# A decoder layer in split fp32: the pool of small tiles is opened last, and three other pools start 8,896 bytes lower

## The chip, the cores and the metric

The kernel runs on one core of a Trainium2 chip. The metric is device time in microseconds (us), from the launch to the end of the program; lower is better. Engine names in the rows: PE is the matmul stream of TensorE, PEld its stream of weight loads, DVE is VectorE, ACT is ScalarE, POOL is GpSimd, SP is SyncE, which issues most DMAs.

## What is computed

One layer of a decoder in float32 for 512 tokens of width 2048. The parts that matter here are the matrix products; every one of them has both operands in on-chip memory (SBUF):

```python
q_a, k_a, v_a, q_b, k_b, v_b = jnp.split(h @ w_in[l], splits, axis=-1)
o_a = swa_sink_attention(q_a, k_a, v_a, sinks[l])       # 16 heads, window 128
o_b = stick_breaking_attention(q_b, k_b, v_b)           # 16 heads, causal
mix = jnp.concatenate([rms(o_a), rms(o_b)], axis=-1) @ w_o[l]
h = layer_norm(ALPHA * h + mix, ln1_g[l], ln1_b[l])
c = memory_cross_attention(h, mem, w_q_mem[l], w_kv_mem[l], w_o_mem[l])
h = layer_norm(ALPHA * h + c, ln2_g[l], ln2_b[l])
gate, up = jnp.split(h @ w_gate_up[l], 2, axis=-1)
f = (jax.nn.silu(gate) * up) @ w_down[l]
h = layer_norm(ALPHA * h + f, ln3_g[l], ln3_b[l])
```

## The kernel before, in words

**Split products.** Each float32 operand is split into a high and a low part of type fp32r (`split`, line 121: ScalarE casts the high part, VectorE subtracts it). A product is then three matmuls, high by high, high by low and low by high (`mm3`, line 143; `product`, line 1032). In each matmul one operand is stationary (128 columns, brought in by a weight load on PEld) and the other one moves through the array (512 or 256 columns). In the rows the moving operand stands first and the stationary one second: `zz<-dn_0h,s2l` is a moving weight tile and a stationary block of activations.

**Stages, in program order.** Values of both attention groups (0 to 120 us; weights move, the input is stationary); attention, with the projections of queries and keys run between its pieces (120 to 530; the input moves, weights are stationary); memory values and keys (530 to 735; 256 columns, weights stationary); the output projection and the values through `w_o_mem` (735 to 1010; weights move); cross-attention (1010 to 1192: `keys` makes a key tile `kq` with `kth` or `ktl` moving and a weight stationary, and `scores` has `kq` move over the stationary hidden state `h1`); its output and the first gate and up blocks (1192 to 1360; weights move); gate and up with seven block products in place of eight (1360 to 2256; weights move); down (2256 to 2686; weights move); and the last layer norm.

**Weight units.** A unit is 128 rows of 4,096 bytes: SP fetches it into a tile `ws`, and `split` makes `wh` and `wl` of it, three buffers of each (pool `pw`). From 735 us on nearly every unit feeds 12 matmuls of 512 columns. Counted from the loops, 7,464 matmuls of 512 columns have a weight tile moving (384 for the values, 768 for `w_o`, 384 through `w_o_mem`, 384 for the output of cross-attention, 5,544 on line 1039), 1,248 have the input moving over a stationary weight tile, and 384 are scores of cross-attention. Of 256 columns there are 2,904: 1,536 for memory, 768 in `keys`, 192 values, 408 in attention.

**What sets the order.** PE and SP run in the order of the program; the order on the other engines comes from the recording layer and its priorities. All waits are on semaphores.

**Where tiles lie.** Pools take their addresses in the order in which they are opened, each after the one before; within a pool each tag has its buffers one after another. The addresses below are bytes within a partition, read from the built programs; the last columns are the first address's remainder on division by 256. Every tile of `px`, `pm`, `pt`, `pg` and `pw` is a multiple of 2,048 bytes long, so all buffers of a pool have the remainder of its first.

| pool (tiles) | first address before | after | remainder before | after |
|---|---|---|---|---|
| `px` (input, `h1`, memory, blocks `a11`, `s2`, ...) | 19744 | 19744 | 32 | 32 |
| `pm` (`kq`, `kth`, values, blocks `a22`, `s1`, ...) | 85280 | 85280 | 32 | 32 |
| `sm` (small tiles and four of 2,048 bytes) | 142624 | 220448 | 32 | 32 |
| `pt` (transposed scores, running sums) | 151520 | 142624 | 224 | 32 |
| `pg` (queries and keys, `ktl`, weight sums) | 176096 | 167200 | 224 | 32 |
| `pw` (`ws`, `wh`, `wl`) | 192480 | 183584 | 224 | 32 |

Of the kernel before, what the change touches and what calls it, by code (L numbers as in the profile page):

```python
# [62 lines left out]
def layer(ctx, tc, io, out):  # L63
# [4 lines left out]
    const = ctx.enter_context(tc.tile_pool(name="const", bufs=1))  # L68
    px = ctx.enter_context(tc.tile_pool(name="px", bufs=4))
    pm = ctx.enter_context(tc.tile_pool(name="pm", bufs=14))  # L70
    sm = ctx.enter_context(tc.tile_pool(name="sm", bufs=2))
    pt = ctx.enter_context(tc.tile_pool(name="pt", bufs=2))
    pg = ctx.enter_context(tc.tile_pool(name="pg", bufs=4))
    pw = ctx.enter_context(tc.tile_pool(name="pw", bufs=3))
    banks = ctx.enter_context(ExitStack())

    def open_banks(k):
# [1343 lines left out]
```

## Time and profile before

| | us |
|---|---|
| median of three runs (2705.70 to 2710.08) | 2708.28 |
| the profiled execution, its own time | 2712.35 |
| the profiled execution, span from first to last instruction | 2710.6 |
| PE busy | 2614.7 |
| DVE busy | 1921.9 |
| ACT busy | 1204.2 |
| mean granted TensorE clock | 0.984 |

The median is 4.07 us below the profiled execution. A row of the timeline gives the start of an instruction (us from the span's start), its length, its engine, line, operation and operands. Matmuls overlap in the pipeline, so the pace of PE is the distance between starts, not the length of one.

### The profile page before, as it was taken

How to read it: one execution, taken by the hardware profiler on the slowest of the kernel's cores; microseconds unless marked ns; L12 is line 12 of the kernel's file. 1: busy time of each engine (PE TensorE's matmuls, PEld its weight loads, DVE VectorE, ACT ScalarE, POOL GpSimd, SP SyncE). 2: the span in 40 equal slices, each digit the busy share in tenths (PEclk: the TensorE clock that was granted, in tenths of full speed). 3: DMA queues.
4: the chain of work that ended last, by engine and by line, in shares of the span. 5: the costliest groups of instructions: out<-in, count | busy, mean ns of one | idle time of the engine just before them, and what ended most of it. 6: DMA issues, size and time to landing. Idle time of an engine off the chain costs nothing.

```text
span 2710.6 us, 33637 instructions
## 1 busy us (share of the span) xinstructions
PE 2614.7 (96%) x13024; PEld 2158.8 (80%) x13024; DVE 1921.9 (71%) x2223; ACT 1204.2 (44%) x1608; POOL 212.3 (8%) x324
## 2 busy tenths in 40 slices
PE   9999999999999999999998989999999998999995
PEld 7877777799988889988777767777778877888884
DVE  4258888896523564457887878778787767777788
ACT  3246666664411353334544444444455443333332
POOL 0001110110000000000101101011111011000001
PEclk9999999999999999999999989999999999999998
DMA  5322222355742573236745546554554568787662
GB/s 180 102 83 70 75 74 71 101 161 190 241 141 96 197 268 107 92 134 210 229 159 212 206 172 214 189 179 152 189 195 168 182 228 312 265 318 261 254 253 102
DMA packets 131264, 476.58 MB, mean 176 GB/s; under 512 B 16160, under 2 KB 16416, under 8 KB 128672
## 3 DMA queue, kind: packets, MB, share of 16 engines
q1 hardware_dynamic: 107568, 391.58, 42.1%
q0 software_dynamic: 23536, 82.85, 8.3%
q8 instruction: 102, 1.67, 0.2%
q14 instruction: 58, 0.48, 0.1%
HBM read 401.49 MB, written 72.88 MB: 175 GB/s over the span
## 4 chain that ended last, share of the span: by engine, by line
PE 70%; issue 14%; DVE 8%; ACT 3%; DMA 2%; POOL 2%; SPq 0%; POOLq 0%; DVEq 0%; ACTq 0%
PE zz L1039 30%; PE ge L1039 2%; POOL f_d L1151 1%; PE kq L147 1%; PE mvp L146 1%; DVE a L351 1%; PE mvp L148 1%; PE vo L148 1%; PE mvp L147 1%; PE kq L148 1%; PE vo L146 1%; PE vo L147 1%; PE kq L146 1%; PE pjqa L146 1%; PE pjqa L148 1%
## 5 line engine op out<-in xcount | busy, mean ns | idle before, releaser
L122 ACT CAST dn_1h<-dn_1a 128x1024 fp32r<-128x1024 f32 x44 | 46.3, 1052 | 76.9 <-PE zz L1039 75.2
L122 ACT CAST dn_0h<-dn_0a 128x1024 fp32r<-128x1024 f32 x44 | 46.3, 1052 | 73.1 <-PE zz L1039 69.1
L123 DVE TENSOR_TENSOR dn_1l<-dn_1a,dn_1h 128x1024 fp32r<-128x1024 f32 x44 | 53.7, 1221 | 23.2 <-ACT dn_1h L122 23.2
L123 DVE TENSOR_TENSOR dn_0l<-dn_0a,dn_0h 128x1024 fp32r<-128x1024 f32 x44 | 53.3, 1221 | 20.0 <-ACT dn_0h L122 20.0
L1161 POOL DMA_DIRECT2D f_d<-fa x22 | 15.8, 716 | 590.6 <-DVE fa L123 590.6
L1151 POOL DMA_DIRECT2D f_d<-fl x66 | 47.1, 714 | 143.4 <-DVE fl L123 140.8
L351 DVE TENSOR_TENSOR_SCAN a<-ones,nl 128x128 f32<-128x128 f32 (+3 forms) x64 | 49.8, 812 | 10.0 <-POOL nl L348 9.9
L122 ACT CAST fh<-fs 128x512 fp32r<-128x512 f32 x44 | 27.2, 619 | 58.3 <-DVE fl L123 42.5
L1151 POOL DMA_DIRECT2D f_d<-fh x66 | 47.2, 715 | 23.7 <-ACT fh L122 20.7
L348 POOL TENSOR_SCALAR_AFFINE_SELECT nl<-nl 128x256 f32<-128x256 f32 x32 | 19.8, 619 | 346.5 <-DVE nl L347 346.5
L1139 PE MATMUL ftr<-ident,f 128*128 128x128 f32 x176 | 26.3, 288 | 16.8 <-DVE fl L123 16.8
L354 ACT ACTIVATE a<-a 128x256 f32<-128x256 f32 (+3 forms) x32 | 23.7, 739 | 39.9 <-DVE a L353 39.9
L123 DVE TENSOR_TENSOR fl<-fs,fh 128x512 fp32r<-128x512 f32 x44 | 30.3, 688 | 14.6 <-DMA f_d<-fl 10.0
L122 ACT CAST dn_1h<-dn_1b 128x1024 fp32r<-128x1024 f32 x22 | 23.2, 1053 | 38.5 <-PE zz L1039 36.7
L1139 PEld LDWEIGHTS ftr<-ident,f 128*128 128x128 f32 x176 | 22.1, 149 | 21.8 <-issue 18.9
L123 DVE TENSOR_TENSOR wmk_0l<-wmk_0s,wmk_0h 128x1024 fp32r<-128x1024 f32 x16 | 19.6, 1226 | 27.6 <-ACT wmk_0h L122 27.5
L122 ACT CAST dn_0h<-dn_0b 128x1024 fp32r<-128x1024 f32 x22 | 23.2, 1053 | 33.4 <-PE zz L1039 29.8
L146 PE MATMUL mkp<-mh,wmk_0h 128*128 128x256 f32 x128 | 36.4, 284 | 1.3 <-DVE ktl L123 1.3
L420 ACT ACTIVATE sa<-sa,nm 128x256 f32<-128x256 f32 x64 | 32.0, 501 | 12.3 <-DVE nm L418 12.2
L146 PE MATMUL mvp<-mh,wmv_1h 128*128 128x256 f32 x128 | 36.7, 287 | 0.0
L146 PE MATMUL mvp<-mh,wmv_0h 128*128 128x256 f32 x128 | 36.4, 285 | 0.0
L824 POOL DMA_DIRECT2D vo_d<-vos x16 | 8.5, 533 | 350.6 <-ACT n1mv L741 277.1
(2465 smaller groups left out, 9743.7 us busy)
## 6 DMA issues: line engine op xcount, KB each, us to landing
f_d<-fh POOLq DMA_DIRECT2D x66, 256.0 KB, 2.8
f_d<-fl POOLq DMA_DIRECT2D x66, 256.0 KB, 2.8
dn_0s<-in_w_dn SPq DMA_DIRECT2D x33, 512.0 KB, 6.9
dn_1s<-in_w_dn SPq DMA_DIRECT2D x33, 512.0 KB, 5.1
wmv_0s<-in_w_mv SPq DMA_DIRECT2D x16, 512.0 KB, 3.5
wmv_1s<-in_w_mv SPq DMA_DIRECT2D x16, 512.0 KB, 3.3
wmk_0s<-in_w_mk SPq DMA_DIRECT2D x16, 512.0 KB, 3.4
wmk_1s<-in_w_mk SPq DMA_DIRECT2D x16, 512.0 KB, 4.2
```

Source lines behind the costliest of these rows:

```text
L122: nc.scalar.copy(hi, src)
L123: return nc.vector.tensor_tensor(lo, src, f32(hi), op=ALU.subtract)
L146: nc.tensor.matmul(acc, lh, rh, start=first, stop=False)
L147: nc.tensor.matmul(acc, lh, rl, start=False, stop=False)
L148: nc.tensor.matmul(acc, ll, rh, start=False, stop=last)
L348: nc.gpsimd.affine_select(out=nlt[:, :, dg], in_=nlt[:, :, dg], compare_op=ALU.is_gt, fill=0.0, base=0, channel_multiplier=1, pattern=[[0, ...
L351: nc.vector.tensor_tensor_scan(a[:, h, :nk][:, ::-1], ones.to_broadcast([P, nk]), nlt[:, h, :nk][:, ::-1], 0.0, op0=ALU.mult, op1=ALU.add)
L354: nc.scalar.activation(a[:, :, :nk], a[:, :, :nk], AF.Exp)
L420: nc.scalar.activation(s4[:, i], s4[:, i], AF.Exp, bias=nm[:, i:i + 1], accum_out=rs[:, i:i + 1])
L1039: nc.tensor.matmul(acc[:, t], l[:, cs(t, P)], r, start=first and c == 0 and i == 0, stop=last and c == 1 and i == 2, skip_group_check=True)
L1139: nc.tensor.transpose(bank[k][:, cs(t, P)], self.f[:, t, o:o + P], ident)
L1151: nc.gpsimd.dma_start(f_d[chunk, b:b + 2, k].rearrange("b p n -> p b n")[:, :, cs(slot, 256)], f32(pieces(v)))
```

## The change

The line that opens the pool `sm` is moved behind the three pools `pt`, `pg` and `pw`. `sm` is 8,896 bytes long (four tiles of 2,048, and small ones), so these three start 8,896 bytes lower, and `sm` starts 77,824 bytes higher.

```diff
     const = ctx.enter_context(tc.tile_pool(name="const", bufs=1))
     px = ctx.enter_context(tc.tile_pool(name="px", bufs=4))
     pm = ctx.enter_context(tc.tile_pool(name="pm", bufs=14))
-    sm = ctx.enter_context(tc.tile_pool(name="sm", bufs=2))
     pt = ctx.enter_context(tc.tile_pool(name="pt", bufs=2))
     pg = ctx.enter_context(tc.tile_pool(name="pg", bufs=4))
     pw = ctx.enter_context(tc.tile_pool(name="pw", bufs=3))
+    sm = ctx.enter_context(tc.tile_pool(name="sm", bufs=2))
     banks = ctx.enter_context(ExitStack())
```

No instruction is added, taken away or moved: on each of the five engines the two built programs have the same instructions in the same order with the same waits on the same semaphores and values, buffer for buffer. The addresses in the table above are all that differs.

## Rows read from the trace of the kernel before

**Rows 1.** The page's part 1: busy time and share of each engine.

```profile
span 2710.6 us, 33637 instructions
PE 2614.7 (96%) x13024; PEld 2158.8 (80%) x13024; DVE 1921.9 (71%) x2223; ACT 1204.2 (44%) x1608; POOL 212.3 (8%) x324
```

**Rows 2.** Stretches of the span: busy time of each engine, granted clock, DMA.

```profile
core 0: us, PE busy (x) PEld busy (x) DVE busy (x) ACT busy (x) POOL busy (x), PEclk, DMA share, GB/s
0.00:530.00 530.00, 514.91 (x2736) 417.03 (x2737) 372.43 (x540) 274.65 (x496) 39.20 (x73) 0.99 0.28 92
530.00:1010.00 480.00, 478.25 (x2915) 421.24 (x2914) 277.67 (x352) 202.11 (x271) 18.21 (x27) 1.00 0.56 184
1010.00:1192.00 182.00, 182.00 (x1190) 166.69 (x1189) 74.78 (x99) 63.22 (x101) 0.53 (x1) 1.00 0.34 111
1192.00:1360.00 168.00, 165.22 (x747) 132.64 (x746) 134.02 (x180) 86.28 (x118) 11.23 (x18) 1.00 0.64 212
1360.00:2256.00 896.00, 853.18 (x3653) 682.95 (x3654) 703.96 (x710) 414.06 (x458) 106.90 (x153) 0.97 0.54 192
2256.00:2686.00 430.00, 421.10 (x1792) 338.27 (x1790) 340.14 (x315) 159.30 (x158) 26.12 (x45) 0.99 0.69 253
```

**Rows 3.** Timeline of PE where scores end and their use begins.

```profile
1184.69 0.39 PE L146 MATMUL s1a<-kq_6h,h1h 128*128 128x512 f32 x1
...
1192.62 0.39 PE L148 MATMUL s1b<-kq_7h,h1l 128*128 128x512 f32 x1
1192.85 0.39 PE L146 MATMUL pvo_0a<-wvo_0h,pmh 128*128 128x512 f32 x1
...
1195.65 0.39 PE L146 MATMUL pvo_0b<-wvo_0h,pmh 128*128 128x512 f32 x1
```

**Rows 4.** Timeline of PE in the down stage.

```profile
2400.16 0.40 PE L1039 MATMUL zz<-dn_1l,a22h 128*128 128x512 f32 x1
...
2404.82 0.40 PE L1039 MATMUL zz<-dn_1h,a22h 128*128 128x512 f32 x1
```

**Rows 5.** Timeline of PE in the first key projection.

```profile
124.88 0.40 PE L148 MATMUL pjkb<-xh,wkb_0l 128*128 128x512 f32 x1
...
127.92 0.40 PE L146 MATMUL pjkb<-xh,wkb_1h 128*128 128x512 f32 x1
```

**Rows 6.** Timeline of PE at two places of the memory stage, 256 columns.

```profile
599.65 0.28 PE L146 MATMUL mvp<-mh,wmv_0h 128*128 128x256 f32 x1
...
601.35 0.28 PE L146 MATMUL mvp<-mh,wmv_0h 128*128 128x256 f32 x1
...
649.99 0.28 PE L148 MATMUL mkp<-mh,wmk_0l 128*128 128x256 f32 x1
...
651.99 0.28 PE L147 MATMUL mkp<-ml,wmk_0h 128*128 128x256 f32 x1
```

**Rows 7.** Timeline of PE in a `keys` block, 256 columns.

```profile
1107.95 0.29 PE L147 MATMUL kq<-ktl,wmq_1h 128*128 128x256 f32 x1
1108.08 0.28 PE L148 MATMUL kq<-kth,wmq_1l 128*128 128x256 f32 x1
...
1110.33 0.28 PE L146 MATMUL kq<-kth,wmq_1h 128*128 128x256 f32 x1
```

**Rows 8.** Groups of splits on ACT and DVE: count, busy us, mean ns, idle before.

```profile
L122 ACT CAST fh<-fs 128x512 fp32r<-128x512 f32 x44 | 27.2, 619 | 58.3 <-DVE fl L123 42.5 <-DMA f_d<-fh 15.8
L122 ACT CAST xh<-x4s 128x512 fp32r<-128x512 f32 x2 | 1.1, 618 | 0.6 <-DMA x4s<-in_xT 0.6
L123 DVE TENSOR_TENSOR dn_1l<-dn_1a,dn_1h 128x1024 fp32r<-128x1024 f32 x44 | 53.7, 1221 | 23.2 <-ACT dn_1h L122 23.2
L123 DVE TENSOR_TENSOR a22l<-hr,a22h 128x1024 fp32r<-128x1024 f32 x2 | 2.4, 1220 | 0.0
```

**Rows 9.** Waits of PE: total us, times, longest; first and last of 21.

```profile
PE ftr L1139 <- DVE fl L123: 16.8, 8, 3.8
...
PE ge L1039 <- DVE wge_1l L123: 0.2, 1, 0.2
```

## The prediction, made before the changed kernel ran

> **What bounds the kernel now.** I read the busy shares first: PE is busy for 2614.7 of 2710.6 us, the next engine, DVE, for 71% [rows 1]. By stretches PE fills each stage, and its clock is granted in full nearly everywhere [rows 2]. The waits of PE, 21 groups, come to 67.2 us in all [rows 9]. So the time is the number of matmuls times the distance between their starts, plus some 67 us of waits and the last layer norm. The instruction streams are the same in both kernels, so nothing can change but how long an access takes at another address. I therefore went to the timeline of PE and measured the distance between starts where no wait intervenes, in pairs of places that differ in where the operands lie.
>
> What a reader should see there: the distance is not one number. In the scores of cross-attention 35 matmuls of 512 columns take from 1184.69 to 1192.62, 7.93 us, or 226.6 ns each; the very next ones, of the same shape and with no wait between, take 12 steps from 1192.85 to 1195.65, 2.80 us, or 233.3 ns each [rows 3]. In the down stage 20 steps take 4.66 us, 233.0 ns [rows 4]. The clock is not the difference: both were granted full clock, that is 2.4 GHz [rows 2, 3], where 6.67 ns are 16 cycles. Nor is traffic: the cross-attention stretch has a DMA share of 0.34, and the down stretch, no slower than the quiet place at 1192.85, has 0.69 [rows 2]. What does differ is the place of the operands. In the scores both `kq` (pool `pm`) and `h1` (pool `px`) begin at remainder 32 of 256 bytes. In the two slower places the moving weight tile is in `pw`, at remainder 224, and the stationary one at 32. With the roles turned round, input moving at 32 over a weight tile at 224, 13 steps take 3.04 us, 233.8 ns [rows 5]. For 256 columns there are two levels with the same operands' remainders (32 moving, 224 stationary): 15 steps in 1.70 us, 113.3 ns, and 17 in 2.00 us, 117.6 ns [rows 6]; the level changes where other pieces have come between.
>
> **The change part by part.** After it `pw`, `pg` and `pt` begin at remainder 32 like `px` and `pm`, so every matmul with a weight tile has both operands at 32, as the scores have now. The multiples of 128 columns at which the stationary slices begin occur in the scores in the same way.
>
> (a) 7,464 matmuls of 512 columns with weights moving. The granted clock of 0.97 and 0.99 in the last two stretches [rows 2] stands for some 2 x (27 + 4) = 62 us at half clock, 1.2 GHz, room for 130 matmuls or so of 427 ns (512 columns, worked out); these I leave out, and call the rest 7,300. Bounds: 0, if remainders do not matter, and 7,300 x 6.67 ns = 48.7 us of gain, if they run at the pace of the scores; the other side is under the rivals. The nearest row is that of the scores, which have after the change's remainders already [rows 3]. I take 48.7.
>
> (b) 1,248 matmuls of 512 columns with the input moving over weights. At the slow pace of rows 5 they could gain 1,248 x 7 = 8.7 us; between the pieces of attention the same operands reach both levels, as for 256 columns in [rows 6]. I take half, 4.3 us, with ends 0 and 8.7.
>
> (c) 2,904 matmuls of 256 columns. They gain at most 117.6 - 113.3 = 4.3 ns each, 12.5 us [rows 6]. The bound on the other side is in `keys`: there a moving `ktl` at 224, with the next weight load also at 224, takes 130 ns by the two starts, against a mean of 119 over 20 steps [rows 7]; at that price all 2,904 would lose some 12 x 2,904 = 35 us. Remainders both at 32 are those of the scores, not of this row, so I take a gain of 5 us.
>
> (d) The other engines. A split of 512 elements takes ACT 619 ns with all tiles at 32 (`fh`) and 618 with the source at 224 (`xh`); one of 1,024 takes DVE 1221 ns with all at 224 (`dn_1l`) and 1220 with all at 32 (`a22l`) [rows 8]. So the moved tiles cost DVE and ACT nothing, and `sm`, whose remainder stays, nothing either. DMAs into `pw` move the same 4,096 bytes per row, and are ahead of their use; I put them at 0, and what they could cost is in (e).
>
> (e) What is late next. A faster PE meets the waits earlier. In gate and up DVE is busy for 704 of 896 us, 79% [rows 2], and the largest waits of PE are for it [rows 9]. Of the 34 to 35 us that (a) gives in those stages and in down (5,256 matmuls x 6.67 ns) I let a seventh go back into waits: a loss of 5 us, with ends 0 and all 35.
>
> Sum against the profiled execution's own time: 2712.35 - 48.7 - 4.3 - 5 + 5 = 2659.4; the median of the runs lies 4.07 lower than that execution, so **2655 us**, 2.0% faster.
>
> A rule speaks against the whole of (a). The Trainium skill, page "SBUF — State Buffer", section "Specifications (TRN2)", gives the memory 16-byte lines and prices only the crossing to a new line; 32, 224 and 8,896 are multiples of 16, so by it every tile begins at a line's start before and after, and the sum would be zero: 2708 us. The trace does not agree with it as the only rule, since it has 226.6 and 233.3 ns for operands that all begin at a multiple of 16 [rows 3].
>
> **The rivals.** *No change, 2708 us.* The two levels may follow not the remainder but the region: everything in `pw` lies above 192,000 bytes before and above 183,000 after, and the scores are the only long products without an operand in the upper pools. Each slow place fits that as well as it fits the remainder, and no row tells them apart. Against it: the fast level does occur with a weight tile in the upper region, in the first pair of [rows 6], and scores run at one pace whichever buffers of `px` and `pm` they use. Time 2700 to 2712. By the page's rule above this would be the result; the row that contradicts that rule does not exclude the region.
>
> *The gain is swallowed where other engines set the pace, 2684 us.* If gate, up and down are held by DVE and DMA, only the 7,464 - 5,256 = 2,208 other matmuls of (a) gain, 14.7 us, with (b) 4.3 and (c) 5: 24 us in all. For: 79% of DVE and a DMA share of 0.69 [rows 2]. Against: PE is busy for 95% and 98% of those stretches, so it is not being held.
>
> *Slower, 2767 us.* Equal remainders collide: with both streams of PE at the same offset the weight load meets the moving reads, as the pair at 224 in `keys` shows with some 10 to 12 ns more than its neighbours [rows 7], in about half of its cases there. At 10.4 ns in half of all, (7,300 + 1,248 + 2,904) / 2 x 10.4 ns = 59.6 us of loss. It decides from the point where 512 columns come out over 234 ns. Against it: the scores, equal too, have the shortest distance in the trace [rows 3].
>
> **How the numbers follow.** Forecast 0.62; swallowed gain 0.12; no change 0.17; slower 0.09. A measurement of this kernel tells about 0.2%, 5.4 us, from no change. Faster is then 0.74, within 0.2% 0.17, slower 0.09. The forecast's own range: the best ends of (b), (c) and (e) give 4.4 + 7.5 + 5 = 17 us more, 2638; at the other end (b) at 0, (c) at 0 and twice (e) give 2670. The range of 8 in 10 has to take in no change as well: 2638 to 2711.
>
> **What would show it.** Right: in the trace after, the starts on line 1039 stand 226.7 ns apart in the down stage, and those of the first key projection too; 1192.85 to 1195.65 loses its step against the scores before it; DVE and ACT keep 1221 and 619 ns; the waits of PE stay below 75 us. Wrong: 233.3 ns on line 1039 (then it is the region or something else that the address does not touch), over 234 (the collision), or 226.7 ns with waits grown by 25 us or more (the swallowed gain). If 256 columns come out at 128, (c) was of the wrong sign.

## The result: 2674.45 us, 1.3% faster

The changed kernel took 2674.45 us (median; 2672.74 to 2675.12 in 4 runs) against 2708.74 us (2705.70 to 2710.08) for the kernel before on the same chip: ratio 0.9874, 95% interval 0.9857 to 0.9891. The prediction was 2655 us, with a range of 2638 to 2711. The direction and the main step held; the gain was 34 us where 53 had been forecast, and 2674.45 lies outside the 2638 to 2670 that the forecast gave itself and inside the wider range only, which had to take in no change as well. Ratios leave out disturbed executions; there was one below, at 4878.85 us among the ten of the first experiment.

The page after, part 1, with the busy time and share of each engine, answers [rows 1]:

```profile
span 2672.5 us, 33637 instructions
PE 2571.9 (96%) x13024; PEld 2159.3 (81%) x13024; DVE 1918.5 (72%) x2223; ACT 1206.1 (45%) x1608; POOL 212.8 (8%) x324
```

The span is 38.1 us shorter and PE's busy time 42.8 us, with the same number of instructions on every engine; DVE (-3.4) and ACT (+1.9) hardly moved. The next view has the stretches of [rows 2], cut where the same matmuls begin in the changed kernel (columns: us, busy time of each engine with its count, granted clock, DMA share, GB/s):

```profile
core 0: us, PE busy (x) PEld busy (x) DVE busy (x) ACT busy (x) POOL busy (x), PEclk, DMA share, GB/s
0.00:527.50 527.50, 512.39 (x2736) 416.43 (x2737) 371.83 (x540) 274.99 (x496) 39.24 (x73) 1.00 0.28 92
527.50:1001.50 474.00, 473.99 (x2915) 425.29 (x2913) 277.97 (x352) 203.01 (x271) 18.35 (x27) 1.00 0.57 187
1001.50:1184.20 182.70, 182.70 (x1189) 167.36 (x1188) 74.74 (x99) 63.18 (x101) 0.53 (x1) 1.00 0.34 112
1184.20:1348.80 164.60, 161.60 (x747) 132.62 (x745) 133.84 (x180) 86.20 (x118) 11.26 (x18) 1.00 0.65 217
1348.80:2226.90 878.10, 832.03 (x3654) 681.62 (x3655) 702.20 (x710) 414.48 (x458) 107.17 (x153) 0.97 0.55 195
2226.90:2643.40 416.50, 408.76 (x1791) 336.00 (x1789) 334.60 (x308) 159.38 (x156) 26.13 (x45) 1.00 0.70 258
```

In the stretches where most weights of 512 columns move, 6 us (the second, which has the 256 columns of memory too), 17.9 (gate and up) and 13.5 (down) are gone. The third, which is mostly matmuls of 256 columns and the scores, has grown by 0.7 us. The granted clock is within 0.01 of the one before in each.

The timeline of PE (columns: start in us, duration, engine, line, operation) at the places of [rows 3 to 7]:

```profile
122.84 0.39 PE L148 MATMUL pjkb<-xh,wkb_0l 128*128 128x512 f32 x1
...
125.79 0.39 PE L146 MATMUL pjkb<-xh,wkb_1h 128*128 128x512 f32 x1
...
598.01 0.28 PE L146 MATMUL mvp<-mh,wmv_0h 128*128 128x256 f32 x1
...
599.81 0.28 PE L146 MATMUL mvp<-mh,wmv_0h 128*128 128x256 f32 x1
...
649.61 0.28 PE L148 MATMUL mkp<-mh,wmk_0l 128*128 128x256 f32 x1
...
651.65 0.28 PE L147 MATMUL mkp<-ml,wmk_0h 128*128 128x256 f32 x1
...
1099.89 0.28 PE L147 MATMUL kq<-ktl,wmq_1h 128*128 128x256 f32 x1
1100.01 0.28 PE L148 MATMUL kq<-kth,wmq_1l 128*128 128x256 f32 x1
...
1102.29 0.28 PE L146 MATMUL kq<-kth,wmq_1h 128*128 128x256 f32 x1
...
1176.98 0.39 PE L146 MATMUL s1a<-kq_6h,h1h 128*128 128x512 f32 x1
...
1184.91 0.39 PE L148 MATMUL s1b<-kq_7h,h1l 128*128 128x512 f32 x1
1185.14 0.39 PE L146 MATMUL pvo_0a<-wvo_0h,pmh 128*128 128x512 f32 x1
...
1187.86 0.39 PE L146 MATMUL pvo_0b<-wvo_0h,pmh 128*128 128x512 f32 x1
...
2367.41 0.39 PE L1039 MATMUL zz<-dn_1l,a22h 128*128 128x512 f32 x1
...
2371.94 0.39 PE L1039 MATMUL zz<-dn_1h,a22h 128*128 128x512 f32 x1
```

Between each pair lie as many steps as between the same matmuls before. The scores keep their 226.6 ns (35 steps in 7.93 us), and the products behind them now run at that pace: 12 steps in 2.72 us, 226.7 ns against 233.3. In down it is 20 steps in 4.53 us, 226.5 ns against 233.0, and in the first key projection 13 in 2.95 us, 226.9 against 233.8. The 256-column places all run at one pace: 15 steps in 1.80 us, 17 in 2.04, 20 in 2.40, 120 ns in each. That is a little slower than the 113.3, 117.6 and 119 before; the long pair in `keys` (130 ns by the rounded starts, 127 to 128 by the exact ones, in 117 of its 256 cases) is gone.

Groups of splits on ACT and DVE (busy us, mean ns, idle before) and waits of PE (total us, times, longest; the first and the last of 22), which answer [rows 8, 9]:

```profile
L122 ACT CAST fh<-fs 128x512 fp32r<-128x512 f32 x44 | 27.3, 620 | 66.5 <-DVE fl L123 49.6
L123 DVE TENSOR_TENSOR dn_1l<-dn_1a,dn_1h 128x1024 fp32r<-128x1024 f32 x44 | 53.5, 1221 | 19.9 <-ACT dn_1h L122 19.8
```

```profile
PE ftr L1139 <- DVE fl L123: 17.9, 8, 4.0
...
PE zz L1039 <- DVE gu4l L123: 0.2, 1, 0.2
```

620 ns and 1221 ns: the other engines take as long as before. The waits sum to 71.7 us against 67.2.

**Matmul by matmul.** Both kernels issue the same 13,024 matmuls in the same order, so the distances between their starts can be subtracted one by one. I call a step steady if in both kernels it is within a tenth or so of the usual distance, which for 256 columns leaves out the long pairs in `keys`. The span's 38.1 us are then:

| steps | count | before, ns | after, ns | us |
|---|---|---|---|---|
| 512 columns, weights moving, steady | 7,253 | 233.3 | 226.9 | -46.5 |
| 512 columns, input moving over weights (1,086), scores of attention and sums of squares (40), steady | 1,126 | 230.7 | 231.1 | +0.5 |
| 256 columns, steady (67 of them scores of attention) | 2,802 | 117.2 | 119.6 | +6.6 |
| 512 columns, steps with a wait or a slow clock | | | | +3.7 |
| 256 columns, the same, and the long pairs in `keys` (-0.9) | | | | -4.2 |
| scores of cross-attention, transposes, start and end | | | | +1.7 |

### The profile page after: what moved, and what is told of

It reads as the page before. It is cut to its first block, busy times and chain, and to the rows that moved or that the text cites. A ratio compares the mean times of both kernels' runs of the same rounds, so it can differ in the third digit from the quotient of the medians.

```text
span 2672.5 us, 33637 instructions
## 1 busy us (share of the span) xinstructions
PE 2571.9 (96%) x13024; PEld 2159.3 (81%) x13024; DVE 1918.5 (72%) x2223; ACT 1206.1 (45%) x1608; POOL 212.8 (8%) x324
## 3 DMA queue, kind: packets, MB, share of 16 engines
q1 hardware_dynamic: 107568, 391.58, 42.8%
## 5 line engine op out<-in xcount | busy, mean ns | idle before, releaser
L123 DVE TENSOR_TENSOR dn_1l<-dn_1a,dn_1h 128x1024 fp32r<-128x1024 f32 x44 | 53.5, 1221 | 19.9 <-ACT dn_1h L122 19.8
L1139 PE MATMUL ftr<-ident,f 128*128 128x128 f32 x176 | 26.2, 284 | 18.3 <-DVE fl L123 17.9
L148 PE MATMUL mvp<-mh,wmv_0l 128*128 128x256 f32 x128 | 36.3, 283 | 0.0
```

Source lines behind the costliest of these rows:

```text
L123: return nc.vector.tensor_tensor(lo, src, f32(hi), op=ALU.subtract)
L148: nc.tensor.matmul(acc, ll, rh, start=False, stop=last)
L1139: nc.tensor.transpose(bank[k][:, cs(t, P)], self.f[:, t, o:o + P], ident)
```

## The experiments

All kernels below run the instruction streams of the changed kernel; only where tiles lie differs. The small tiles `mx`, `nm`, `rs` (64 bytes each for both buffers), `mv` (128 bytes) and the 32 bytes of `ones` serve as spacers, so that no tile is added. "Apart" is the remainder of 256 at which `pw`, `pg` and `pt` start, less that of `px` and `pm`. The kernels ran on several chips; each ratio is to the kernel before on the same chip, whose median lay between 2705.34 and 2708.74 us.

**Region or remainder.** The first four kernels ask whether the place (region) or the remainder counts, and whether the remainder itself or the equality of two remainders. The first leaves the large pools within 192 bytes of where the change put them, and makes the remainders those of before:

```
     pm = ctx.enter_context(tc.tile_pool(name="pm", bufs=14))
+    s0 = ctx.enter_context(tc.tile_pool(name="s0", bufs=2))
     pt = ctx.enter_context(tc.tile_pool(name="pt", bufs=2))
...
-            mx = sm.tile([P, 4], F32, tag="mx", name=f"mx{j}_{st}")
+            mx = s0.tile([P, 4], F32, tag="mx", name=f"mx{j}_{st}")
```

with `nm` and `rs` likewise.

> 192 bytes of small tiles stand between the pools pm and pt, so pt, pg and pw begin at remainder 224 of 256 as in the kernel before, at addresses only 192 bytes above those of the changed kernel; instructions and waits are the same. Theory 1 (remainder): 512 columns with weights moving go back to 233.3 ns, 256 columns to 117 to 118, time 2709 us within 5. Theory 2 (region: the 8,896 bytes themselves or the place of the small tiles matter): 226.7 ns and 2674 us as in the changed kernel.

Measured: 2705.62 us, ratio to the kernel before 0.9999 (0.9989 to 1.0010). The whole gain is gone. The timeline of PE in the down stage, at the matmuls of [rows 4]:

```profile
2400.59 0.39 PE L1040 MATMUL zz<-dn_1l,a22h 128*128 128x512 f32 x1
...
2405.26 0.39 PE L1040 MATMUL zz<-dn_1h,a22h 128*128 128x512 f32 x1
```

20 steps in 4.67 us: 233.5 ns. 192 bytes decide, not 8,896, and the region rival falls.

The next three put all the large pools at one remainder: 128, by opening `const` behind them,

```
-    const = ctx.enter_context(tc.tile_pool(name="const", bufs=1))
     px = ctx.enter_context(tc.tile_pool(name="px", bufs=4))
...
     pw = ctx.enter_context(tc.tile_pool(name="pw", bufs=3))
+    const = ctx.enter_context(tc.tile_pool(name="const", bufs=1))
     sm = ctx.enter_context(tc.tile_pool(name="sm", bufs=2))
```

then 224, with `ones` and `nsink` in a small pool ahead of `px`, and 0, with `gq` and `nsink` there.

> The pool of constants is opened behind the large pools too, so px, pm, pt, pg and pw all begin at remainder 128 of 256, the start of a 64-byte piece, instead of 32; instructions and waits are the same. Theory 1a (equal remainders of both operands make the fast pace): 226.7 ns for 512 columns, 120 ns for 256, 2674 us. Theory 1b (what costs is a start inside a 64-byte piece, and the rest of 13 ns over 512 columns at 2.4 GHz comes from it): 512 columns at 220 ns or less, some 45 us or more below the changed kernel, 2630 us or less.

> All large pools, px and pm too, begin at remainder 224; instructions and waits are the same. Theory 1a (equal remainders make the fast pace): 226.7 ns for 512 columns and 2674 us. Theory 1c (an operand at 224 costs by itself, because 32 bytes are left to the next multiple of 128 or 256): 233.3 ns or more for 512 columns and 2709 us or more.

> All large pools begin at remainder 0; instructions and waits are the same. Theory 1a (equal remainders): 226.7 ns and 2674 us, as with 32 and 128. Theory 1b (a start inside a 64-byte piece costs): the same as with 128, 220 ns or less and 2630 us or less. If 0 and 128 differ from each other by more than 5 us, the unit is 256 bytes and not 64.

Measured: 2672.74 us (ratio 0.9869, 0.9854 to 0.9885) at 128, 2675.02 (0.9880, 0.9864 to 0.9896) at 224, 2672.88 (0.9872, 0.9856 to 0.9889) at 0. All three are the changed kernel again, so theories 1b (a start inside a 64-byte piece costs) and 1c (224 costs by itself) fall. With every operand at 224, the same down steps:

```profile
2369.62 0.39 PE L1040 MATMUL zz<-dn_1l,a22h 128*128 128x512 f32 x1
...
2374.16 0.39 PE L1040 MATMUL zz<-dn_1h,a22h 128*128 128x512 f32 x1
```

4.54 us for 20 steps, 227 ns. No remainder is good or bad by itself; that the operands have the same one is what counts. The 256 columns too behave as after in all three (119.5 ns).

**Which distance.** The next kernels put spacers of several sizes between the two groups of pools: `mx` (64), `mv` (128), `mv`, `mx` and `nm` (256), `ones` (32), and `mx`, `nm`, `rs` and `ones` (224), with the edit of the first kernel, or for `ones`

```
-    ones = const.tile([P, 1], F32, name="ones")
+    ones = s0.tile([P, 1], F32, name="ones")
```

One more kernel puts 192 bytes before `pw` alone:

```
     pg = ctx.enter_context(tc.tile_pool(name="pg", bufs=4))
+    s0 = ctx.enter_context(tc.tile_pool(name="s0", bufs=2))
     pw = ctx.enter_context(tc.tile_pool(name="pw", bufs=3))
```

> The two tiles of row maxima (64 bytes) lie between the pool of m-tiles and the pools of keys, scores and weights, which therefore start 64 bytes higher than in the changed kernel: remainder 96 of 256 against 32 of the other operand. Theory 1 (equal remainders of 256 make the fast pace, any difference the slow one): 233.3 ns for 512 columns and about 2706 us, as before. Theory 2 (the difference 192 is a bad one among good ones): 226.7 ns and about 2673 us. Theory 3 (only differences that are multiples of 64 at larger scale matter): 226.7 ns as well, so this run alone does not part it from theory 2.

> 128 bytes (the four tiles of mean and variance) between the two groups of pools: remainder 160 against 32. Theory 1 (equal remainders of 256 wanted): 233.3 ns and about 2706 us. If the period is 128 and not 256: 226.7 ns for 512 columns, 120 ns for 256 columns, about 2673 us.

> 256 bytes between the two groups (mean and variance, row maxima and their negatives): remainder 32 against 32, but 256 bytes apart in the 2,048 bytes that one row of a half tile covers, where they were equal in the changed kernel. Theory 1 with a period of 256: 226.7 ns and about 2673 us, as the changed kernel. If the period is larger (512 or 2,048): another pace, 233.3 ns and about 2706 us if any difference is slow.

> The 192 bytes of row statistics stand before the pool of weights alone: weights at remainder 224, keys, queries and transposed scores at 32 like the input and the m-tiles. If the pair weights against input or m-tiles decides (it makes 7,271 of the 7,464 matmuls of 512 columns and all of the projections), the 512-column stages go at 233.3 ns, the time is 2700 to 2706 us, and only the 408 matmuls of 256 columns between transposed scores and m-tiles stay at 120 ns. If what counted were where keys and transposed scores lie, the time is about 2675 us.

> The 32 bytes of ones lie between the two groups of pools instead of below both: input and m-tiles at remainder 0, weights, keys and transposed scores at 32. If the pace follows the distance of the remainders (226.7 ns at 0, about 229.5 at 64, 232.5 at 128, 233.3 at 192), 512 columns go at 227 to 229.5 ns and the time is 2673 to 2681 us, 256 columns at 116 to 120 ns. If equality alone is fast and every other distance is on the slow side, about 2681 to 2706 us.

> Both pieces (192 bytes of row statistics, 32 of ones) lie between the groups: input and m-tiles at remainder 0, weights, keys and transposed scores at 224, which is 32 bytes short of equal the other way round. If the distance counts the short way round the 256, as at 32: the same pace as with 32 apart. If it counts how far the moving operand lies ahead (64, 128, 192: slower and slower), 233 ns and about 2706 us.

Measured, with the mean of the steady steps (512 columns with weights moving; 256 columns):

| apart | us | ratio (95%) | 512, ns | 256, ns |
|---|---|---|---|---|
| 0 (changed kernel) | 2674.45 | 0.9874 (0.9857 to 0.9891) | 226.9 | 119.6 |
| 256 | 2674.96 | 0.9882 (0.9863 to 0.9901) | 226.9 | 119.6 |
| 64 | 2680.54 | 0.9907 (0.9883 to 0.9930) | 229.1 | 116.2 |
| 128 | 2706.59 | 1.0003 (0.9992 to 1.0014) | 232.8 | 118.9 |
| 192 (first kernel) | 2705.62 | 0.9999 (0.9989 to 1.0010) | 233.3 | 117.0 |
| 192, `pw` alone | 2705.94 | 1.0003 (0.9993 to 1.0013) | 233.3 | 117.3 |
| 224 | 2709.26 | 1.0008 (0.9999 to 1.0017) | 233.2 | 117.4 |
| 32 | 2710.95 | 1.0015 (1.0005 to 1.0025) | 233.3 | 117.9 |

The down steps again, first with `pw` alone moved:

```profile
2391.28 0.39 PE L1040 MATMUL zz<-dn_1l,a22h 128*128 128x512 f32 x1
...
2395.94 0.39 PE L1040 MATMUL zz<-dn_1h,a22h 128*128 128x512 f32 x1
```

with 64 bytes between the groups:

```profile
2372.42 0.39 PE L1040 MATMUL zz<-dn_1l,a22h 128*128 128x512 f32 x1
...
2377.00 0.39 PE L1040 MATMUL zz<-dn_1h,a22h 128*128 128x512 f32 x1
```

with 32:

```profile
2397.73 0.40 PE L1040 MATMUL zz<-dn_1l,a22h 128*128 128x512 f32 x1
...
2402.40 0.40 PE L1040 MATMUL zz<-dn_1h,a22h 128*128 128x512 f32 x1
```

and with 256:

```profile
2366.83 0.39 PE L1040 MATMUL zz<-dn_1l,a22h 128*128 128x512 f32 x1
...
2371.36 0.39 PE L1040 MATMUL zz<-dn_1h,a22h 128*128 128x512 f32 x1
```

4.66, 4.58, 4.67 and 4.53 us for 20 steps: 233, 229, 233.5 and 226.5 ns. At 64 neither time that had been expected came (2706 or 2673 us), and at 32 the time, 2710.95 us, lies above both ranges. Four things follow. 256 bytes apart is as good as 0, so the remainder of 256 is enough; a period of 512 or more is excluded, and one of 128 or 64 by the kernels at 128 and 64. The weights against input and `m`-tiles are the pair that sets the time: with `pw` alone moved it is 2705.94 us, so where keys and transposed scores lie, which few of these products have as an operand, adds nothing that the time shows. The expected law "the nearer the remainders, the faster" does not hold: 32 is as slow as 192, and 64 one way (229.1) is not 64 the other way (192: 233.3). And the 256 columns go the other way: equal remainders are their slowest case, 64 apart their fastest. Why 64 differs stays open.

**Which pair of operands.** While one matmul streams, the weights of the next are fetched. In the changed kernel's down stage a weight load of 0.19 us begins with each matmul and brings in the stationary operand of the one after it (`a22l` while `a22h` is in use):

```profile
2367.41 0.39 PE L1039 MATMUL zz<-dn_1l,a22h 128*128 128x512 f32 x1
2367.41 0.19 PEld L1039 LDWEIGHTS zz<-dn_1h,a22l 128*128 128x128 f32 x1
```

To tell whether a stream is compared with its own stationary operand or with the next one, one kernel moves the low halves of the weights and of two input slots (`xl0` and `xl1`, later `a11l`, `a12l` and others) to 224 together; `low` is set from the tile's name, and `wl` moves in the same way at its other two places:

```
...
-        return px.tile(shape, dt, tag=f"x{half}", name=name)
...
+        if half == 0 and low:
+            return pxl.tile(shape, dt, tag="x0l", name=name)
+        if half == 0:
+            return pxh.tile(shape, dt, tag="x0h", name=name)
+        return px.tile(shape, dt, tag="x1", name=name)
...
-        lo = pw.tile([P, 1024], F32R, tag="wl", name=f"{name}l")
+        lo = pwl.tile([P, 1024], F32R, tag="wl", name=f"{name}l")
```

`pxl` and `pwl` are opened behind 192 bytes of spacer, after all other large pools.

> The low halves of the weights and the low halves of the first two input tiles (later h1l0, h1l1, a11l, a12l) are moved together to remainder 224; everything else, the high halves too, lies at 32. In mm3 the weights' high half (32) moves over the high half, the low half (224) over the high half, the high half over the low half (224), and while each of these streams, the weights of the next are fetched: high, low, high. Theory A (what counts is a stream against the stationary operand that it is multiplied by): in products with these tiles as stationary operand one pair of three is equal, so 2 in 3 run slow (mean about 231 ns); with the other stationary tiles, all at 32, 1 in 3 (mean about 229); some 1,700 and 5,760 matmuls, +7.6 and +12.9 us, about 2695 us. Theory B (what counts is a stream against the stationary operand of the next matmul, fetched meanwhile): with these tiles all pairs are equal, 226.7 ns; with the others 1 in 3 differs, about 229; about 2687 us.

Measured: 2688.09 us, ratio 0.9936 (0.9919 to 0.9952). The total is nearer to B's number, but the timeline of PE, which has both cases side by side in the down stage, is not; first a product with `a12`, then the one behind it with `a22`:

```profile
2520.53 0.40 PE L1048 MATMUL zz<-dn_1h,a12h 128*128 128x512 f32 x1
2520.76 0.40 PE L1048 MATMUL zz<-dn_1l,a12h 128*128 128x512 f32 x1
2521.00 0.39 PE L1048 MATMUL zz<-dn_1h,a12l 128*128 128x512 f32 x1
...
2528.93 0.40 PE L1048 MATMUL zz<-dn_1h,a12h 128*128 128x512 f32 x1
...
2531.26 0.39 PE L1048 MATMUL zz<-dn_1l,a22h 128*128 128x512 f32 x1
2531.49 0.39 PE L1048 MATMUL zz<-dn_1h,a22l 128*128 128x512 f32 x1
2531.72 0.39 PE L1048 MATMUL zz<-dn_1h,a22h 128*128 128x512 f32 x1
...
2540.87 0.39 PE L1048 MATMUL zz<-dn_1l,a22h 128*128 128x512 f32 x1
```

With `a12` 36 steps take 8.40 us, 233.3 ns; with `a22`, 42 take 9.61 us, 229 ns. For `a12` every stream has the remainder of the next stationary operand, and B wanted 226.7 ns: B falls. It is so throughout gate, up and down: 1,559 steady steps with `a11` or `a12` take 233.1 ns, the 3,836 with the other blocks 229.1. Own pairs differ in 2 of 3 there and in 1 of 3 with `a22`. That fits A in order, not in size: 1 in 3 gives the mean (229), but 2 in 3 is as slow as all (233.3, where A said 231). The kernel before has that case too: of the three matmuls of each round in `wo`, the one over a `pt` tile (`mixl`, from the third unit on) had 224 against 224, and steps there took 233.3 ns on average. Here 24 steps take 5.60 us in the kernel before:

```profile
803.87 0.39 PE L146 MATMUL wo1a<-wo_4h,mixh 128*128 128x512 f32 x1
804.10 0.40 PE L147 MATMUL wo1a<-wo_4l,mixh 128*128 128x512 f32 x1
804.33 0.40 PE L148 MATMUL wo1a<-wo_4h,mixl 128*128 128x512 f32 x1
...
809.47 0.39 PE L146 MATMUL wo1a<-wo_5h,mixh 128*128 128x512 f32 x1
```

A comparison with the operand two places on would give the same counts as A, so what is shown is that the next one is not it; that it is the matmul's own pair is the reading that is left, not shown against that other one. The total, 14.6 us of span above the changed kernel, is 22.5 us from the 512 columns (230.0 against 226.9 ns), less 5 from the 256 columns (117.8 against 119.6) and some 3 from other steps, which is how it came near B's number by another way.

No version here beats the changed kernel by more than the spread of its executions (2672.74 us at 128 is the lowest median). 64 apart in the stages of 256 columns alone would be worth some 3.6 us there by the stage times (attention with the memory values 523.6 against 525.0 us, memory keys 91.3 against 92.2, keys and scores 183.4 against 184.7), less than the 5.4 us that the prediction takes a measurement to tell; the pools are shared with the other stages. It wasn't tried.

## Why the prediction was right, and where it was off

- **What bounds the kernel: right.** PE's pace between starts set the time, and the time followed it in eleven further kernels.
- **(a), 48.7 us: right in mechanism and size.** 46.5 us, 6.4 ns on each of 7,253 steps. The scores [rows 3] had the after-state in the trace before, and every weight product took their pace. The rivals "no change" by region and the swallowed gain fell: 192 bytes took the whole gain back, and gate, up and down alone gave 31.4 us of it. The 62 us at half clock are room for 145 matmuls of 427 ns, not 130; with 7,253 steady ones against the 7,300 taken, nothing hangs on it. The prediction's wording was a remainder of 32 for both; the kernels at 0, 128 and 224 show that the common value is free.
- **The rule of 16-byte lines.** By the Trainium skill, "SBUF — State Buffer", "Specifications (TRN2)", SBUF has 16-byte lines and each cross to a new line pays a penalty; if that were all, tiles that start on such a line should cost the same wherever they lie. Moving three pools by 32 bytes against the others changed 226.9 ns into 233.3. What a single access pays no run here shows; the rule alone does not give the pace of PE.
- **(b), -4.3 us: wrong, +0.5.** The uninterrupted projection of [rows 5] did speed up, to 226.9 ns. But that projection is one unbroken run of 105 matmuls, with 104 steady steps (233.4 to 226.9 ns, -0.7 us). The other 982 steady steps of the group stand in runs of 3 to 30 between pieces of attention; they took 230.4 ns before, not 233.8, and 231.6 after (+1.2 us). One unbroken row was taken for the group, though the next sentence of the prediction says that between the pieces both levels occur; why the pieces change the pace stays open. The term was 4.8 us off.
- **(c), -5 us: wrong sign, +6.6.** I saw two levels (113.3 and 117.6) at the same remainders and let equal remainders move the pace toward the lower one, as with 512 columns. They do not: equal gives 120, above both. The prediction named 128 ns as what would show the sign wrong; it was wrong at 120 already. (With the 117 long pairs counted in, the steady steps lose 5.7 us and not 6.6.) The step at fault is carrying a pace from 512 columns to 256; 11.6 us.
- **(d), 0: right.** 620 and 1221 ns.
- **(e), +5 us: right.** Waits rose by 4.5 us, to 71.7. Not foreseen: 4.2 us less in the other steps of 256 columns, 2.4 of them in memory keys and 0.9 the long pairs.
- **The collision, slower: fell.** All at 224 runs at 227 ns, and the long pair in `keys` goes at 120. In the short matmuls equal remainders do cost 2.4 ns, against the 10.4 that that rival took.
- **The subtraction at the end: 4 us off.** The profiled execution of before was 3.6 us above its median (2712.35 against 2708.74); that of after was not (2674.17 against 2674.45). Taking the same 4.07 off the forecast assumed that it would be.

The terms add up. (a) is 2.2 us short, (b) 4.8, (c) 11.6, and the subtraction 4.3; the last three rows of the table, forecast as +5 in (e), came to +1.2, which is 3.8 the other way. That makes 19.1 of the 19.45 us between 2655 and 2674.45.

## What to carry to other kernels

Where PE bounds a kernel and its weights change at every matmul, compare the distance between starts with the addresses of both operands: a spacer of a few bytes, or the order in which pools are opened, can be worth over 1%. For products like these (fp32r, new weights for each matmul) give the moving and the stationary operands of the 512-column ones the same remainder of 256 bytes, and look at the shapes one by one, since a shorter one can want the opposite. And when one term is read from an undisturbed stretch, count how many of its instructions run undisturbed before multiplying.

## What the runs showed that was not expected

- Two operands that each may lie at 0, 32, 128 or 224 of 256 without harm cost 2.8% per matmul of 512 columns (233.3 against 226.9 ns) when they lie 32 or 192 apart.
- For 256 columns the sign is reversed: 119.6 ns equal, 116.2 with 64 apart, 117.0 with 192.
- 64 bytes apart gives a third pace, 229.1 ns, in which steps of 226, 229 and 232 ns take turns; a product with one unequal pair in three shows 229 ns as well, and one with two in three the full 233.3.
- The splits on VectorE and ScalarE take as long at either place: 1221 ns for `dn_1l` before and after, 619 and 620 ns for `fh`.
